# Modulation dots on VectorE, and the operand splits, stores and squares of two stages rearranged, in a two-block fp32 kernel

## The chip, the cores and the metric

The kernel runs on one core of one Trainium2 chip. The time is that of one execution on the device, in microseconds; shorter is better. Beside the runs without a profile there is one profiled execution, from which every instruction's start and duration is known.

## The reference, cut to what matters

Two blocks follow each other on an input of 1024 rows (time) by 1024 channels, all in fp32. In the first block a vector c modulates the normalised input, one projection feeds three branches (pooling, a short convolution, a long convolution), and the branches are gated, summed and projected:

```python
mod = (c_act @ w_ada + b_ada)[:, None, :]
shift, scale, gate = jnp.split(mod, 3, axis=-1)
u = layer_norm(x) * (1 + scale) + shift
proj = u @ w_in + b_in
...
y_a = y_a * pool_scale * jax.nn.silu(a_g)
y_b = b_b * causal_dwconv(b_c * b_h, sc_w, sc_b) * jax.nn.silu(b_g)
h_c = causal_dwconv(c_a * jax.nn.sigmoid(c_b), cf_w, cf_b)
y_c = jax.nn.silu(layer_norm(h_c, cf_ln_g, cf_ln_b)) * jax.nn.silu(c_g)
g_m = jax.nn.sigmoid(merge).reshape(bsz, slen, N_BRANCH, D_MODEL)
m = (g_m[:, :, 0] * (y_a @ w_branch[0])
     + g_m[:, :, 1] * (y_b @ w_branch[1])
     + g_m[:, :, 2] * (y_c @ w_branch[2]))
out = m @ w_out
return layer_norm(ALPHA * x + gate * out, ln_g, ln_b)
```

The second block (attention and a spatial gate) is not touched, except for the last product of its conv-gated MLP, which closes the program:

```python
gate, val = jnp.split(zc, 2, axis=-1)
return (jax.nn.silu(gate) * val) @ w_down
```

Here the gated value is 1024 by 2816, so it is 22 tiles of 128 channels, and `w_down` is 2816 by 1024.

## The kernel before, in words

**Products.** Every fp32 product is made of three TensorE products of split operands. `hilo` casts an operand to a short form on ACT (the hi part, line 165) and subtracts that from the operand on DVE (the lo part, through `tt`, line 159). `mm3` (through `mul`, line 143) then issues hi by hi, hi by lo and lo by hi. One weight tile of 128 channels needs 2 halves of 512 columns by 8 k-tiles by 3 products, 48 matmuls. `act` (line 156) is any ACT function, `stt` (line 162) a fused DVE operation, `flip` (line 146) a transposition on TensorE.

**Order.** The program is a list of slots, written by hand. For each slot the instructions are issued in the order `pre`, `mm`, background tasks (as many from the queue `bgq` as the slot's number `bg` says), `epi`. Each engine and each DMA queue works through its own instructions in this order and waits where a semaphore says so. Weights come through SP's queue into tiles `wr` (two of them, line 247) and are split into `wh` and `wl` some slots ahead (`dma_ahead`, `split_ahead`). A tile name with a ring (`bufs`) is given out again when its last reader is done; the instruction that fills it, a DMA's issue too, waits for that.

**Start** (`start`, from line 552). The input is normalised into eight tiles (`ln_norm`, line 604). Then, for each k-tile of 128 channels, `dot(k)` forms two values per channel, shift and scale, as a row of `w_ada` times the vector, summed: the first with a multiply on POOL (line 644) and a sum and a bias on ACT (`dot_sum`), the second with one DVE instruction (`ada_dot`, line 542, which takes product and sum together, and a second short instruction that reads the accumulator). `prep(k, h)` transposes half h of the k-tile, makes u on ACT and splits it into tiles of U (the names `A` in the profile, line 661 for the cast), and `mac` multiplies three weights by it.

**Long convolution** (`conv_tasks`). A channel tile's 31 taps run on DVE beside the products of later tiles, from p, the gated and padded input, into h. `stats` then stores h, squares it on ACT into an `e` tile (a ring of two, `n_e`; later of one), and two accumulating DMAs on POOL's queue add h and the square into hs and hq. The `e` tiles are used by the epilogues as well (`epi_store`: an activation from PSUM into `e` and a store on SP).

**Passage to the branches.** After the pooling products (`pool_slot(3)` to `pool_slot(0)`, with projection tiles for the merge gates between) the memory of the pool stage is given back (`open_q`) and the branch stage begins. Before its first product it needs y of the second branch: eight tiles from HBM (`yb_sp`), each split (`split_y`) into the big buffers B0 and B1. The first four are fetched to free places when the last paired projection ends (`end`), the last four in `open_q` through tiles `ld` (line 1043). The last two merge tiles leave through `epi_store` (line 836), pool 0's two results through tiles `s`.

**Branches** (`branch(n, d, bg)`). Twenty-four products, n in the order 1, 0, 2, of one weight tile each. The epilogue multiplies PSUM by the gate tile g (a ring of three, loaded from `mg_sp` one branch ahead by `load_g`), adds the sum so far from HBM (`mi<-m_sp`) and stores it on SP (`m_sp<-g`, line 1163), except in the last round. Background tasks make the dots for the gate (first four) and the y tiles of the next n (`prep_y`).

**Second projection** (`down`, from line 1956). The 2816 by 1024 product is done by seven products of half-size blocks in place of eight (Winograd's form of Strassen's scheme). With W1 and W2 the upper and lower 11 tiles of `w_down`, S and T are sums of blocks, of the gated value and of the weights. Seven products p, in the order 1, 5, 2, 6, 7, 3, 4, have 11 units each, one for each k-tile f, and each unit is 12 matmuls (4 banks by 3). For unit u, `step(u)` issues `prep(u + 3)` (sums on DVE, then the split of x and y), `load_sum(u + 9)` (DMAs that fill or accumulate T, the accumulating ones on POOL's queue), `load(u + 7)` (on SP: y into a ring `yr` of four, line 2018, and a tile of the gated value `A<-g_sp`, line 2024), one of the eight loads of the residual x2 in units 13 to 20 (`B<-x_sp`, line 2122), and two background tasks. Four units after a product ended `results(p)` queues its DVE additions into x2 and w, five for each of four banks for p = 6.

Of the kernel before, what the change touches and what calls it, by code (L numbers as in the profile page):

```python
# [22 lines left out]
P = 128  # L23
# [83 lines left out]
class Kernel:  # L107
# [437 lines left out]
    def start(self):  # L545
# [4 lines left out]
        def first():  # L550
# [72 lines left out]
            self.split_ahead(1)  # L623
            dot_sum(0)
            prep(0, 0)
# [7 lines left out]
            dot(1)  # L633
            dot_sum(1)
            prep(1, 0)
# [5 lines left out]
        def dot(k):  # L641
            if k < NK:
                w = st["ada"][2 * k]
                nc.gpsimd.tensor_tensor(w, w, st["cb"], ALU.mult)
                self.ada_dot(8 + k, st["ada"][2 * k + 1], st["cb"])

        def dot_sum(k):
            w, m = st["ada"][2 * k], self.mod[:, k:k + 1]
            self.act(w, w, AF.Identity, accum=m)
            self.act(m, m, AF.Identity, bias=self.par("b_ada", k))  # L650

# [20 lines left out]
        def mm(*ws):  # L672
            steps = [(k, h) for k in range(1, NK) for h in range(2)]
            for i, s in enumerate(steps):
                if i + 2 < len(steps):
                    k, h = steps[i + 2]
                    if h == 0:
                        dot_sum(k)
                    prep(k, h)
                    if h == 0:  # L680
                        dot(k + 1)
                if s[0] < NK - 1:
                    for j in range(3):
                        mac(*s, j)
# [26 lines left out]
    def block1(self):  # L711
# [8 lines left out]
        def conv_tasks(j, p):  # L720
# [10 lines left out]
            def stats():  # L731
                h = T["h"]
                nc.sync.dma_start(h_sp[j], h)
                sq = e_tile()
                self.act(sq, h, AF.Square)
# [96 lines left out]
        def epi_store(ct, func, sp, i):  # L832
            def one(ps, k):
                e = e_tile()
                self.act(e, ps, func, bias=self.bias_in(ct + k))
                nc.sync.dma_start(sp[i + k], e)
            return lambda x, y: [Task(0, lambda: one(x, 0)),
                                 Task(0, lambda: one(y, 1), 4 if self.n_e == 1 else 0)]
# [118 lines left out]
        def pool_slot(g):  # L957
            s = {}

            def pre():  # L960
                while self.bgq:
                    self.bgq.popleft()()
                pairs.flush()
                if g == 0:
                    self.open_right("ws")
                    self.resume()
                    self.dma_ahead()
                    for j in range(4):
                        split_y(1, j)
                    self.split_ahead(1)  # L970
# [13 lines left out]
            def one(c):  # L984
                if g:
                    e = e_tile()
                else:
                    e = self.c1.tile([P, 1040], F, tag="s", name="s", bufs=2)[:, 0:1024]
                self.act(e, s["ps"][c], AF.Identity, scale=self.par("pool_scale", 2 * g + c))
                (nc.sync if g else nc.gpsimd).dma_start(ya_sp[2 * g + c], e)  # L990

            def epi():
                pairs.todo = [Task(0, lambda c=c: one(c), c + 1) for c in range(2)]
                if g == 0:
                    pairs.flush()

# [51 lines left out]
        def open_q():  # L1048
# [8 lines left out]
            T["cb"] = self.c1.tile([P, 1024], F, name="cb2")  # L1057
            for j in range(4, 8):
                load_y(1, j)
            for j in (1, 2):  # L1060
# [50 lines left out]
        def branch(n, d, bg):  # L1111
# [37 lines left out]
            def epi():  # L1149
# [12 lines left out]
                else:  # L1162
                    nc.sync.dma_start(m_sp[d], g)

# [5 lines left out]
        for n in (1, 0, 2):  # L1170
            for d in range(8):
                branch(n, d, 2 if n == 1 else 1)
                if n == 1 and d in (1, 2):
# [790 lines left out]
    def down(self):  # L1964
# [42 lines left out]
        def load(u):  # L2007
# [5 lines left out]
            y = T  # L2013
            if p == 7:
                y = st["T3"][u % 6]
            elif p in (1, 2, 3):
                y = st["ring"].tile([P, H], F, tag="yr", name="yr", bufs=4)
                fetch(y, {1: W1[:, lo], 2: W2[:, lo], 3: W2[:, hi]}[p])
            g = None
# [7 lines left out]
        def load_sum(u):  # L2027
# [6 lines left out]
            if p == 5:  # L2034
                fetch(T, W1[:, lo])
                more(T, W1[:, hi])
# [7 lines left out]
        def prep(u):  # L2044
# [14 lines left out]
            out = []  # L2059
            for x, n in ((src, "x"), (y, "y")):  # L2060
                t = [st["ring"].tile([P, H], R, tag=n + c, name=n + c, bufs=PREP + 1) for c in "hl"]
                self.hilo(*t, x)
                out.append(t)
            st["op", u] = out

# [9 lines left out]
        def results(p):  # L2075
# [6 lines left out]
            for b in range(4):  # L2082
# [7 lines left out]
                elif p == 6:  # L2090
                    add(w, ps, ALU.subtract)
                    add(t21, ps)
                    add(t21, p1)
                    add(t12, w)
                    add(t22, w)
                else:
                    o, op, t, cs = {2: (t11, ALU.add, b, lo), 7: (t22, ALU.subtract, 4 + b, hi),
                                    3: (t12, ALU.add, b, hi), 4: (t21, ALU.add, 4 + b, lo)}[p]
                    add(o, ps, op)
                    tasks.append(lambda t=t, cs=cs: store(t, cs))  # L2100
            if p == 6:
                tasks[:] = tasks[0::5] + tasks[1::5] + tasks[2::5] + tasks[3::5] + tasks[4::5]
            return tasks

        def step(u):
            p, f = units[u]

            def pre():
# [9 lines left out]
                if u == half + 2:  # L2118
                    st["x"] = self.big("B0", F)
                if half + 2 <= u < half + 10:  # L2120
                    t = u - half - 2
                    nc.sync.dma_start(st["x"][:, t], self.x2_sp[t])
# [106 lines left out]
```

## Time and profile before

| | us |
|---|---|
| median of three runs (2690.15 to 2691.99) | 2691.73 |
| the profiled execution's own time | 2690.44 |
| its span, first to last instruction | 2688.6 |
| PE busy | 2618.4 |
| DVE busy | 1861.9 |
| ACT busy | 980.6 |
| POOL busy | 157.4 |

In the profile PE is TensorE, DVE VectorE, ACT ScalarE, POOL GpSimd and SP the engine that issues most DMAs. A row of a timeline has start, duration, engine, line, operation, output<-input, shape and count; a bracket at its end says how long the engine stood idle before it and what released it. A row of windows has the stretch, its length, PE's busy time with the number of matmuls, the granted TensorE clock as a share of full speed, the mean busy share of the DMA engines and the rate in GB/s. A row of waits has who waited, for whom, the total in us, how often, and the longest. The stages by time are: start to 48, projections and the long convolution to about 577, then the pool stage, passage 1023 to 1062, branches from there to about 1310, the second block, and the second projection from 2453 to the end.

### The profile page before, as it was taken

The page shows a single profiled execution, that of the slowest core. Times are in us where ns is not written, and L with a number is a line of the kernel's source. Part 1 is how long each engine was busy: PE and PEld are TensorE (multiplying, and loading weights), DVE is VectorE, ACT ScalarE, POOL GpSimd, SP SyncE. Part 2 cuts the span into 40 slices and gives each one's busy share as a digit, 9 for nine tenths or more (in the row PEclk, how much of TensorE's full clock was granted, in tenths as well). Part 3 has the DMA queues.
Part 4 walks back from the last instruction along what each step waited for, and adds up shares of the span by engine and source line. Part 5 has one row for each costly group of instructions (what it writes and reads, how often), then busy time and mean ns, then how long its engine had stood idle before and what let it go on. Part 6 is the DMA issues. An engine that isn't in the chain of part 4 may idle for free.

```text
span 2688.6 us, 29545 instructions
## 1 busy us (share of the span) xinstructions
PE 2618.4 (97%) x11688; PEld 2142.2 (80%) x11688; DVE 1861.9 (69%) x2141; ACT 980.6 (36%) x1284; POOL 157.4 (6%) x178
## 2 busy tenths in 40 slices
PE   5999999999999998999999999999999999999998
PEld 3888888888888886877787788888788888887786
DVE  7788988989887664666474255536637788885576
ACT  6322233333343343222243255542323334343333
POOL 4000000000000000000042100000000000000220
PEclk9999999999999998999999999999999999999999
DMA  6112232232242225776432122113532222217964
GB/s 236 55 63 79 79 102 86 102 102 102 94 164 98 98 103 206 278 288 234 134 134 87 63 79 79 55 32 119 177 116 79 86 93 72 94 55 239 274 151 147
DMA packets 104396, 331.97 MB, mean 123 GB/s; under 512 B 11713, under 2 KB 12225, under 8 KB 104258
## 3 DMA queue, kind: packets, MB, share of 16 engines
q1 hardware_dynamic: 95474, 309.65, 32.6%
q0 software_dynamic: 8784, 20.45, 4.1%
q8 instruction: 91, 1.49, 0.2%
q14 instruction: 47, 0.39, 0.0%
HBM read 247.21 MB, written 75.50 MB: 120 GB/s over the span
## 4 chain that ended last, share of the span: by engine, by line
PE 63%; issue 15%; DMA 9%; DVE 9%; ACT 3%; SPq 1%; POOL 1%; DVEq 0%; ACTq 0%; POOLq 0%
PE pp L143 61%; DMA ld<-h_sp 1%; DVE h L162 1%; DMA A<-g_sp 1%; DMA B<-x_sp 1%; DMA hs<-h 1%; DVE wl L159 1%; DVE g L159 1%; PE pm L143 1%; DVE A L159 1%; PE pp L146 1%; DVE sums L159 1%; PE pm L146 1%; DVE B L159 1%; DMA adag<-in_ada 1%
## 5 line engine op out<-in xcount | busy, mean ns | idle before, releaser
L143 PE MATMUL pp<-A,wh 128*128 128x512 f32 x2432 | 769.6, 392 | 14.3 <-DVE A L159 9.1
L143 PEld LDWEIGHTS pp<-A,wh 128*128 128x128 f32 x2432 | 454.4, 188 | 116.2 <-DVE A L159 10.9
L143 PE MATMUL pp<-A,wl 128*128 128x512 f32 x1296 | 506.0, 390 | 1.8 <-DVE wl L159 1.8
L143 PE MATMUL pp<-B,A 128*128 128x512 f32 x1676 | 487.7, 390 | 1.2 <-DVE B L159 1.1
L143 PE MATMUL pp<-A,w 128*128 128x512 f32 x1664 | 439.6, 390 | 2.8 <-ACT two L456 1.3
L143 PE MATMUL pp<-B,w 128*128 128x512 f32 x1136 | 374.7, 389 | 0.0
L143 PEld LDWEIGHTS pp<-B,A 128*128 128x128 f32 x1676 | 313.9, 188 | 68.0 <-DVE B L159 2.3
L143 PEld LDWEIGHTS pp<-A,w 128*128 128x128 f32 x1664 | 311.7, 188 | 70.6 <-DVE pp L159 3.8
L162 DVE SCALAR_TENSOR_TENSOR h<-p,par_t,h 128x1024 f32<-128x1024 f32 x240 | 308.6, 1286 | 4.7
L143 PEld LDWEIGHTS pp<-A,wl 128*128 128x128 f32 x1296 | 243.8, 188 | 54.2 <-DVE wl L159 3.5
L143 PE MATMUL pp<-B,wh 128*128 128x512 f32 x800 | 264.7, 395 | 14.3 <-ACT B L165 6.6
L159 DVE TENSOR_TENSOR wl<-wr,wh 128x1024 fp32r<-128x1024 f32 (+1 forms) x120 | 142.5, 1188 | 177.5 <-ACT wh L165 173.8
L143 PEld LDWEIGHTS pp<-B,w 128*128 128x128 f32 x1136 | 213.2, 188 | 44.2
L143 PEld LDWEIGHTS pp<-B,wh 128*128 128x128 f32 x800 | 151.4, 190 | 48.8 <-ACT B L165 7.4
L165 ACT CAST wh<-wr 128x1024 fp32r<-128x1024 f32 (+1 forms) x120 | 118.5, 989 | 187.6 <-PE pp L143 158.1
L162 DVE SCALAR_TENSOR_TENSOR z<-pp,par_t,z 128x1023 f32<-128x1023 f32 x88 | 112.6, 1280 | 48.3 <-ACT z L156 47.3
L143 PE MATMUL pp<-yh,xh 128*128 128x512 f32 x308 | 122.3, 397 | 7.1 <-ACT yh L165 7.1
L143 PE MATMUL pp<-A,A 128*128 128x512 f32 x324 | 126.6, 391 | 0.9 <-DVE A L159 0.6
L143 PE MATMUL pp<-yl,xh 128*128 128x512 f32 x308 | 122.8, 399 | 3.9 <-DVE yl L159 3.8
L143 PE MATMUL pp<-B,wl 128*128 128x512 f32 x320 | 126.0, 394 | 0.0
L373 ACT CAST w<-raw 128x1024 fp32r<-128x1024 f32 x50 | 52.6, 1053 | 200.5 <-PE pp L143 148.5
L143 PE MATMUL pp<-yh,xl 128*128 128x512 f32 x308 | 121.2, 394 | 0.0
(278 smaller groups left out, 3150.8 us busy)
## 6 DMA issues: line engine op xcount, KB each, us to landing
raw<-in_w_in SPq DMA_DIRECT2D x66, 512.0 KB, 4.1
wr<-in_w_in SPq DMA_DIRECT2D x63, 512.0 KB, 3.5
raw<-in_w_up SPq DMA_DIRECT2D x34, 512.0 KB, 5.3
mg_sp<-e SPq DMA_DIRECT2D x24, 512.0 KB, 4.2
wr<-in_w_br SPq DMA_DIRECT2D x24, 512.0 KB, 6.0
g<-mg_sp SPq DMA_DIRECT2D x24, 512.0 KB, 5.6
A<-g_sp SPq DMA_DIRECT2D x44, 256.0 KB, 6.2
g_sp<-z SPq DMA_DIRECT2D x21, 512.0 KB, 3.0
```

Source lines behind the costliest of these rows:

```text
L143: return self.nc.tensor.matmul(*a, **k)
L146: self.nc.tensor.transpose(*a)
L159: return self.nc.vector.tensor_tensor(out, a, b, op)
L162: self.nc.vector.scalar_tensor_tensor(out, a, s, b, op0, op1)
L165: self.nc.scalar.copy(hi, src)
L373: self.nc.scalar.copy(t.__dict__[which][0], src)
```

## The change

It has three parts.

*Start.* `dot(k)` is now two `ada_dot` on DVE; the POOL multiplies, the ACT sums and `dot_sum` go.

*Convolution to branches.* The square of h goes into p, whose taps are done, and no longer into an `e` tile. In `epi_store` the last two merge tiles use an `e` and an `s` tile, and their stores go to POOL's queue. In `pool_slot(0)` the splits of y 0 to 3 are issued ahead of the last pair's epilogues, the four late y tiles are loaded right after the first weights into the big buffer A0, which is free by then, and pool 0's two epilogues write to A0 and become background tasks of the first branch (its `bg` is 4). The stores of m in `branch` go to POOL's queue.

*Second projection.* Product 1 fetches its y straight into T, so that product 5 no longer fetches the same W1 tile again. The x2 loads move from units 13 to 20 to units 20 to 27. `prep` splits y ahead of x. Product 6's results are 12 additions instead of 20: four (adding w to t12) move to product 3's results, and four (adding p1 to t21) to product 2's.

```diff
@@ start @@
         def dot(k):
             if k < NK:
-                w = st["ada"][2 * k]
-                nc.gpsimd.tensor_tensor(w, w, st["cb"], ALU.mult)
-                self.ada_dot(8 + k, st["ada"][2 * k + 1], st["cb"])
+                for n in range(2):
+                    self.ada_dot(8 * n + k, st["ada"][2 * k + n], st["cb"])
-
-        def dot_sum(k):
-            w, m = st["ada"][2 * k], self.mod[:, k:k + 1]
-            self.act(w, w, AF.Identity, accum=m)
-            self.act(m, m, AF.Identity, bias=self.par("b_ada", k))
...
@@ stats @@
-                sq = e_tile()
+                sq = p[:, 0:1024]
@@ epi_store @@
-                e = e_tile()
+                last = sp is mg_sp and i == 22
+                if last and k:
+                    e = self.c1.tile([P, 1040], F, tag="s", name="s", bufs=2)[:, 0:1024]
+                else:
+                    e = e_tile()
                 self.act(e, ps, func, bias=self.bias_in(ct + k))
-                nc.sync.dma_start(sp[i + k], e)
+                (nc.gpsimd if last else nc.sync).dma_start(sp[i + k], e)
@@ pool_slot @@
+                if g == 0:
+                    for j in range(4):
+                        split_y(1, j)
                 pairs.flush()
                 if g == 0:
                     self.open_right("ws")
                     self.resume()
                     self.dma_ahead()
-                    for j in range(4):
-                        split_y(1, j)
+                    t = T["free"] = self.big("A0", F)
+                    for j in range(4, 8):
+                        T["ld"][1, j] = t[:, j]
+                        nc.sync.dma_start(t[:, j], yb_sp[j])
...
-                    e = self.c1.tile([P, 1040], F, tag="s", name="s", bufs=2)[:, 0:1024]
+                    e = T["free"][:, c]
...
                 if g == 0:
-                    pairs.flush()
+                    self.bgq.extend(pairs.todo)
+                    pairs.todo = []
@@ open_q @@
-            for j in range(4, 8):
-                load_y(1, j)
@@ branch @@
-                    nc.sync.dma_start(m_sp[d], g)
+                    nc.gpsimd.dma_start(m_sp[d], g)
...
-                branch(n, d, 2 if n == 1 else 1)
+                branch(n, d, 4 if n == 1 and d == 0 else 2 if n == 1 else 1)
@@ down: load, load_sum @@
-            if p == 7:
+            if p == 1:
+                fetch(T, W1[:, lo])
+            elif p == 7:
                 y = st["T3"][u % 6]
-            elif p in (1, 2, 3):
+            elif p in (2, 3):
...
             if p == 5:
-                fetch(T, W1[:, lo])
                 more(T, W1[:, hi])
@@ down: prep @@
-            for x, n in ((src, "x"), (y, "y")):
+            for x, n in ((y, "y"), (src, "x")):
@@ down: results @@
                     add(t21, ps)
-                    add(t21, p1)
-                    add(t12, w)
                     add(t22, w)
...
+                    if p == 3:
+                        add(o, w)
                     add(o, ps, op)
                     tasks.append(lambda t=t, cs=cs: store(t, cs))
+                    if p == 2:
+                        add(t21, p1)
@@ down: step @@
-                if half + 2 <= u < half + 10:
-                    t = u - half - 2
+                if 2 * half - 2 <= u < 2 * half + 6:
+                    t = u - 2 * half + 2
```

How the instructions move on an engine is shown at three places, as line, operation, output<-input and shape. First DVE in the start, right after the last normalisation, before; `A_201<-u` is the lo part of u, `B_161` a tile of `w_ada`:

```order
L542 ISA B_161,mod<-B_161,cb,bada_76 128x1024
L542 ISA mod 128x1
L159 TENSOR_TENSOR wl<-wr,wh 128x1024
L159 TENSOR_TENSOR A_201<-u,A_202 128x512
L159 TENSOR_TENSOR wl<-wr,wh 128x1024
L159 TENSOR_TENSOR A_201<-u,A_202 128x512
L159 TENSOR_TENSOR w2l<-w_164,w2h 128x1024
L542 ISA B_161,mod<-B_161,cb,bada_76 128x1024
```

and the same place now:

```order
L542 ISA B_161,mod<-B_161,cb,par_t 128x1024
L542 ISA mod 128x1
L542 ISA B_161,mod<-B_161,cb,bada_76 128x1024
L542 ISA mod 128x1
L159 TENSOR_TENSOR wl<-wr,wh 128x1024
L159 TENSOR_TENSOR A_201<-u,A_202 128x512
L159 TENSOR_TENSOR wl<-wr,wh 128x1024
L159 TENSOR_TENSOR A_201<-u,A_202 128x512
L159 TENSOR_TENSOR w2l<-w_164,w2h 128x1024
L542 ISA B_161,mod<-B_161,cb,par_t 128x1024
```

Each k has one more dot on DVE, ahead of the lo parts. Second ACT at the passage, before; `raw` and `sums` hold y 0 to 3, `ld` y 4 to 7, `wh<-wr` are branch weights:

```order
L156 ACTIVATE e<-pp,par_t 128x1024 x2
L165 CAST B_6558<-raw 128x1024 x2
L165 CAST B_6558<-sums 128x1024 x2
L165 CAST wh<-wr 128x1024 x2
L156 ACTIVATE s<-pp,par_t 128x1024 x2
L165 CAST B_6558<-ld 128x1024 x4
```

and now, with y 4 to 7 in `A_6544`:

```order
L165 CAST B_6520<-raw 128x1024 x2
L165 CAST B_6520<-sums 128x1024 x2
L156 ACTIVATE e<-pp,par_t 128x1024
L156 ACTIVATE s<-pp,par_t 128x1024
L165 CAST wh<-wr 128x1024 x2
L165 CAST B_6520<-A_6544 128x1024 x4
L156 ACT_TABLE_LOAD
L156 ACTIVATE cb_6596<-cb_6596 128x1024
L156 ACTIVATE A_6544<-pp,par_t 128x1024 x2
```

The casts of y come ahead of the two merge epilogues, and pool 0's two epilogues behind the casts of the late tiles. Third DVE in the second projection where product 3 is prepared, before; `B_16323` is x2, `A_15809` S and `A_16008` the memory of g, p1 and w:

```order
L159 TENSOR_TENSOR A_15809<-A_15809,A_16008 128x512
L159 TENSOR_TENSOR xl<-A_15809,xh 128x512
L159 TENSOR_TENSOR yl<-yr,yh 128x512
L159 TENSOR_TENSOR B_16323<-B_16323,A_16008 128x512 x2
L159 TENSOR_TENSOR A_15809<-A_15809,A_16008 128x512
```

and now:

```order
L159 TENSOR_TENSOR A_15780<-A_15780,A_15972 128x512
L159 TENSOR_TENSOR yl<-yr,yh 128x512
L159 TENSOR_TENSOR xl<-A_15780,xh 128x512
L159 TENSOR_TENSOR B_16272<-B_16272,A_15972 128x512 x2
L159 TENSOR_TENSOR A_15780<-A_15780,A_15972 128x512
```

The split of y now lies between the sum and the split of x.

More of the change, by code (lines that the diff above doesn't have):

```diff
@@ L623, in first @@
             self.split_ahead(1)
-            dot_sum(0)
             prep(0, 0)
@@ L633, in first @@
             dot(1)
-            dot_sum(1)
             prep(1, 0)
@@ L676, in mm @@
                     k, h = steps[i + 2]
-                    if h == 0:
-                        dot_sum(k)
                     prep(k, h)
@@ L2013, in load @@
             y = T
-            if p == 7:
+            if p == 1:
+                fetch(T, W1[:, lo])
+            elif p == 7:
                 y = st["T3"][u % 6]
-            elif p in (1, 2, 3):
+            elif p in (2, 3):
                 y = st["ring"].tile([P, H], F, tag="yr", name="yr", bufs=4)
-                fetch(y, {1: W1[:, lo], 2: W2[:, lo], 3: W2[:, hi]}[p])
+                fetch(y, W2[:, lo if p == 2 else hi])
             g = None
@@ L2063, in prep @@
                 out.append(t)
-            st["op", u] = out
+            st["op", u] = out[::-1]
         def macs(u, banks):
@@ L2098, in results @@
                                     3: (t12, ALU.add, b, hi), 4: (t21, ALU.add, 4 + b, lo)}[p]
+                    if p == 3:
+                        add(o, w)
                     add(o, ps, op)
                     tasks.append(lambda t=t, cs=cs: store(t, cs))
-            if p == 6:
-                tasks[:] = tasks[0::5] + tasks[1::5] + tasks[2::5] + tasks[3::5] + tasks[4::5]
+                    if p == 2:
+                        add(t21, p1)
+            if p in (2, 6):
+                tasks[:] = tasks[0::3] + tasks[1::3] + tasks[2::3]
             return tasks
```

## The prediction

> **What bounds the kernel now.** The page's first part comes first, because it says which engine could be the bound at all.
>
> ```profile
> span 2688.6 us, 29545 instructions
> PE 2618.4 (97%) x11688; PEld 2142.2 (80%) x11688; DVE 1861.9 (69%) x2141; ACT 980.6 (36%) x1284; POOL 157.4 (6%) x178
> ```
>
> PE (TensorE) is busy for 2618.4 of 2688.6 us, so about 70 us of idle time, and some time at a reduced clock, is all that a change can win which leaves PE's work alone; this one does (11688 matmuls before and after). The second view is PE's busy time by stretches, cut where PE stands still.
>
> ```profile
> core 0: us, PE busy (x), PEclk, DMA share, GB/s
> 0.00:48.00 48.00, 17.60 (x44) 1.00 0.84 329
> 1023.00:1062.00 39.00, 25.63 (x88) 0.82 0.64 230
> 1140.00:1240.00 100.00, 96.93 (x423) 1.00 0.78 284
> 2513.00:2541.00 28.00, 21.49 (x73) 0.88 1.04 305
> 2541.00:2615.00 74.00, 74.00 (x328) 1.00 0.67 151
> 2615.00:2655.00 40.00, 35.93 (x140) 1.00 0.65 181
> ```
>
> In 2541:2615 PE never waits: 74.00/328 = 0.2256 us is the floor of a 512-column matmul. What a stretch loses is its length less its matmuls by that: 1023:1062 loses 39 − 88 × 0.2256 = 19.1, 1140:1240 4.6, 2513:2541 11.5, 2615:2655 8.4 us. The first 48 us hold little PE work. The change touches each of these five places, so the rest of the trace was read there, in the timeline and in the waits.
>
> **Start (dots on DVE).** The rows are from the timelines of POOL, DVE, ACT and PE; the column after the start is the duration.
>
> ```profile
> 20.71 11.68 POOL L644 TENSOR_TENSOR B<-B,cb 128x1024 f32<-128x1024 f32 x4
> 19.22 0.80 DVE L604 TENSOR_SCALAR B<-B,sm 128x1024 f32<-128x1024 f32 x1
> 20.78 2.82 DVE L604 TENSOR_SCALAR B<-B,sm 128x1024 f32<-128x1024 f32 x1 [0.77 <-POOL sm L601]
> 42.21 3.37 DVE L542 CUSTOM_DVE_ANT_0 B<-B,cb,bada 128x1024 f32<-128x1024 f32 x1
> 47.17 0.69 DVE L159 TENSOR_TENSOR A<-u,A 128x512 fp32r<-128x512 f32 x1 [1.58 <-ACT A L661]
> 47.78 1.28 DVE L542 CUSTOM_DVE_ANT_0 B<-B,cb,bada 128x1024 f32<-128x1024 f32 x1
> 45.71 0.78 ACT L156 ACTIVATE u<-pm,mod 128x512 f32<-128x512 f32 x1 [12.67 <-DVE mod L542]
> 39.04 0.79 PE L143 MATMUL pp<-A,wh 128*128 128x512 f32 x1 [4.39 <-DVE A L159]
> 47.91 0.50 PE L143 MATMUL pp<-A,wh 128*128 128x512 f32 x1 [0.23 <-DVE A L159]
> ```
>
> While POOL multiplies (from 20.71, without a gap for eight tiles), the same DVE dot takes 3.37 us that takes 1.28 once POOL is done, and the last normalisation takes 2.82 against 0.80. With the multiplies gone POOL runs nothing there, so I take the short durations for every DVE instruction of the start.
>
> Now the chain with short durations. The last normalisation ends at 20.78 + 0.80 = 21.6; two dots of k = 0 at 1.28 end by 24.2. ACT then makes u (0.78), its cast (about 0.62), two weight casts (about 1.04 each) and the second half: 28.8. DVE has wl, ul, wl, ul and w2l between, each as soon as its cast is there, and ends w2l at 30.0; the two dots of k = 1 end at 32.6, u and cast at 34.0, ul at 34.7. PE has 18 matmuls and 8 transposes of k = 0 from 26.3 on; at a pitch of 0.43 us (the rows from 39 to 43 us are twice as slow as the floor) it is done at about 36.5. So the first matmul of k = 1 moves from 47.9 to about 37: a gain of **10.5** (8 to 12, as PE's clock is slow for more or less of it). Beyond it PE has 18 matmuls and 8 transposes per k, about 5 us, and DVE 2 × 1.28 + 2 × 0.69 = 3.9: two dots instead of one still hide under PE. What they cost if not is 0.2 us a k.
>
> **Squares into p.** After the last merge tiles of the convolution part an epilogue waits for a tile that the accumulating DMA of the squares still reads.
>
> ```profile
> 575.08 1.11 ACT L156 ACTIVATE e<-pp,par_t 128x1024 f32<-128x1024 f32 x1 [4.56 <-DMA hq<-e]
> 576.72 3.02 PE L143 MATMUL pp<-A,w 128*128 128x512 f32 x12 [1.33 <-ACT two L456]
> ```
>
> Squares no longer take an e tile, so the 4.56 us on ACT go, and with them PE's 1.33. The tile p they now hold is not written again until the next channel's gating, some 60 us later, which covers the accumulating DMA (the waiter above found it late by 4.56 us only). Gain **1.3** (0 to 1.5).
>
> **Passage to the branches.** SP, ACT, DVE and PE in the order of their start:
>
> ```profile
> 1028.93 4.18 SPq L836 DMA_DIRECT2D mg_sp<-e  x2
> 1033.21 8.45 SPq L247 DMA_DIRECT2D wr<-in_w_br  x4
> 1042.23 10.28 SPq L1043 DMA_DIRECT2D ld<-yb_sp  x4
> 1032.67 1.98 ACT L165 CAST B<-raw 128x1024 fp32r<-128x1024 f32 x2
> 1037.73 1.05 ACT L165 CAST wh<-wr 128x1024 fp32r<-128x1024 f32 x1 [1.19 <-DMA wr<-in_w_br]
> 1051.86 1.04 ACT L165 CAST B<-ld 128x1024 fp32r<-128x1024 f32 x1 [9.79 <-DMA ld<-yb_sp]
> 1052.93 1.23 DVE L159 TENSOR_TENSOR B<-ld,B 128x1024 fp32r<-128x1024 f32 x1 [11.62 <-ACT B L165]
> 1038.83 1.22 PE L143 MATMUL pp<-B,wh 128*128 128x512 f32 x2 [6.33 <-ACT wh L165]
> 1052.95 0.79 PE L143 MATMUL pp<-B,wh 128*128 128x512 f32 x1 [5.66 <-ACT B L165]
> 1061.59 0.62 PE L143 MATMUL pp<-B,wh 128*128 128x512 f32 x2
> ```
>
> PE ends pool 0 at 1038.83 − 6.33 = 1032.5 and waits for the first branch weight, whose DMA stood on SP behind the two merge stores. It waits again, 5.66 us, for y tile 4 of 8, because the four late y loads can be issued only after pool 0 has been stored out of the memory they land in. Between them it runs at half clock (0.82 in the row of the stretch). With the stores on the GpSimd queue SP is free from about 1018: weights land near 1022, the y loads go into A0, free when the last merge product has read it (about 1027), and land from 1030 to 1036 at the pace of the y loads above.
>
> On ACT the four casts of y 0 to 3 come first (B free at 1023.3, so 4 × 1.0 to 1027.5), then two epilogues (1.1 each) to 1030, two weight casts to 1032, four casts of the late tiles to 1036. DVE follows with 1.23 a tile: y lo 1032.5, weights lo 1033.7 and 1034.9, late tiles 1039.7. PE ends pool 0 at 1032.5, waits 0.9 for the first wl, then runs 48 matmuls of branch 1.0 in 10.8: 1044.2, where before branch 1.1 began at 1061.59, the last row. That is 17.4; I take **17** (13 to 18.5: 13 if the y loads land at the 10.28 us pace above from a start 4 us later, 18.5 if no weight wait is left).
>
> **Stores of m on the GpSimd queue.** The landing times of the stores and loads of tile ya_sp (min/median/max; its longest, 8.7, is of the two stores that POOL issues), and a DMA row of the page, whose last number is the median to landing:
>
> ```profile
> DMA to landing us min/median/max: 2.6/4.6/8.7
> g<-mg_sp SPq DMA_DIRECT2D x24, 512.0 KB, 5.6
> ```
>
> The sixteen stores wait on SP for each branch's sum, and loads queue behind them; in 1140:1240 PE loses 4.6 us, mostly for y products whose loads came late. Without the stores SP reaches its loads up to a branch earlier. I take **2.5** (4.5 if all of it goes, −2 if landings like the 8.7 hold g tiles now and then). The Trainium skill, page "DMA: Bandwidth & Descriptors", section "Issuing engines are not separate DMA queues", speaks against this: all issuers share the same 16 DMA engines, and only issue time is saved; by it, if the late loads of this stretch are late by bandwidth, the term is 0 and the time 2642.5. The DMA share of 0.78 there, below the 1.04 of 2513:2541, is why I don't take it so.
>
> **Second projection.** Seven products of 11 units each, 12 matmuls a unit, 2.71 us at the floor. The first two rows are the x2 loads (tile x_sp from 2480 to 2550) and their landing; then ACT's waits from 2510 to 2540, one wait of PE, and the DVE timeline of product 3.
>
> ```profile
> L2122 SPq DMA_DIRECT2D B<-x_sp x8: 319/320/320, 2491.3 to 2525.9; - x8
> DMA to landing us min/median/max: 12.0/15.0/15.7
> ACT xh L165 <- DMA A<-g_sp: 19.0, 6, 4.9
> 2517.79 0.50 PE L143 MATMUL pp<-yh,xh 128*128 128x512 f32 x1 [1.04 <-ACT yh L165]
> 2630.08 0.69 DVE L159 TENSOR_TENSOR xl<-A,xh 128x512 fp32r<-128x512 f32 x1 [0.76 <-ACT xh L165]
> 2630.69 0.68 DVE L159 TENSOR_TENSOR yl<-yr,yh 128x512 fp32r<-128x512 f32 x1
> 2631.29 1.29 DVE L159 TENSOR_TENSOR B<-B,A 128x512 f32<-128x512 f32 x2
> 2632.50 0.69 DVE L159 TENSOR_TENSOR A<-A,A 128x512 f32<-128x512 f32 x1
> ```
>
> *Product 2* (2513:2541) is DMA-bound: a DMA share of 1.04 at 305 GB/s, and loads wait in a full queue (x2 tiles land after 15 us, ACT waits 19.0 us for g). Ahead of that point the change takes away 11 × 256 KB (W1 read once) and moves eight x2 loads of 512 KB behind it by seven units: 7 MB, at 305 GB/s 23 us of transfer, against 11.5 lost. The loads for products 6 and 7 behind it have slack in 2541:2615 (0.67). I take **11.3** (6 if half the stall stays behind the accumulating DMAs, 11.9).
>
> *Product 3* loses 8.4 to 8.7. Here DVE is in a cycle: 0.76 idle until x is cast, then from start to start xl 0.61, yl 0.60, two adds 1.21 and the sum for the next unit 0.69, together 3.87 a unit. With y split first, yl fills the idle time: 3.26 with two adds, 2.05 with none, and 8 of the 20 adds leave product 6's results, so only some six units carry two. 6 × (3.26 − 2.71) = 3.3 us of lag stays within the three units (8 us) prepared ahead. Gain **8.5** (6 to 8.7). Product 1's y straight into T saves its two short stalls: **0.9** (0 to 1).
>
> **Sum.** 10.5 + 1.3 + 17 + 2.5 + 11.3 + 8.5 + 0.9 = 52.0. The profiled execution took 2690.44 (span 2688.6 and 1.84 around it): 2690.4 − 52.0 = 2638.4. The median of the runs is 2691.73, 1.3 above it: 2639.7, predicted **2640.0**. A difference of 0.2%, 5.4 us, is what a measurement tells from no change.
>
> **Rivals.** (a) The passage is partly given back: with branch 1.0 done at 1044, branch 1.2 needs gate tiles and the sums of h, loaded on SP behind everything else; if they come at the old distance, PE stalls about 8 us there: 2648. For it: cb and ada loads stood after 1055 before; against it: by my chain they land near 1046, 4 us ahead of need. Chance 0.12. (b) In product 2 the accumulating DMAs, not the bytes, set the pace, and half the stall stays: 2646. The share above 1 in 2513:2541 speaks for bytes. Chance 0.12. (c) POOL's multiplies do not slow DVE; then DVE gains nothing at the start and the two dots in a row replace one: term 0 to 2, 2649. Against it stand 3.37 and 1.28. Chance 0.06. (d) The slower side: m's stores on POOL's queue land late. The g ring has three tiles, so a load of g waits on SP for the store three branches back, with branch weights behind it. Three branches are 3 × 48 × 0.2256 = 32.5 us; less a load of 5.6 and two DVE steps of 1.23, a store may take 24 us. At 40 us each third branch is 16 us late: 16 × 16/3 = 85 lost, 2725. At about 34 the loss is 52 and the time unchanged. The slowest known landing, 8.7, is far from that. The Trainium skill, page "SBUF — State Buffer", section "Who interferes with whom", names a way to it: a DMA issued by GpSimd can be starved by VectorE of the port time in which its descriptors are made; no row here but the 8.7 bears on it. Slower 0.03, same 0.02. The forecast itself has 0.65.
>
> All the upper ends of the terms give 12 + 1.5 + 18.5 + 4.5 + 11.9 + 8.7 + 1 = 58.1, so 2633.6; (a) and (b) together 2654. Range **2633.0 to 2656.0**. All cases but (d) are faster: 0.95 faster, 0.02 same, 0.03 slower.
>
> **What would show it.** Right: DVE dots of 1.3 us from 21.6 on and the first k = 1 matmul near 37; one PE wait of about 1 us after pool 0 and branch 1.1 near 1044 less the 12 us won before; no PE wait in product 2, and a DVE cycle under 3.3 us in product 3. Wrong: long dots without POOL, PE waits for gate tiles in branch 1.2, ACT still waiting for g in product 2, m_sp landings above 20 us.

## The result, and the profile after

The changed kernel takes 2631.66 us (median of four runs, 2631.33 to 2632.98) against 2690.94 us for the kernel before beside it. The ratio is 0.9783, 95% interval 0.9768 to 0.9799: 59.3 us less. Forecast were 2640.0 us and a range from 2633.0, so the direction and the order of size were right, and the time lies 1.3 us below the range. The page after begins so:

```profile
span 2629.8 us, 29512 instructions
## 1 busy us (share of the span) xinstructions
PE 2599.1 (99%) x11688; PEld 2139.3 (81%) x11688; DVE 1855.9 (71%) x2157; ACT 972.5 (37%) x1260; POOL 144.0 (5%) x188
```

PE has the same 11688 matmuls. Its busy time is 19 us less all the same: a matmul that runs slowly counts with its longer duration, and the stretches with a granted clock of 0.82 and 0.88 are gone. The stretches that lost time before, now (the bounds have moved with the time won):

```profile
core 0: us, PE busy (x), PEclk, DMA share, GB/s
0.00:38.00 38.00, 18.57 (x51) 1.00 0.95 372
1005.00:1030.00 25.00, 23.75 (x104) 1.00 0.70 261
1030.00:1106.00 76.00, 76.00 (x338) 1.00 0.90 331
1106.00:1206.00 100.00, 100.00 (x443) 1.00 0.78 283
2470.00:2490.00 20.00, 20.00 (x90) 1.00 1.01 324
...
2564.00:2596.00 32.00, 32.00 (x143) 1.00 0.83 260
```

From 1030 on PE is busy without a gap in each of them, and the clock is 1.00 in all rows. The DMA share beside product 2 (2470:2490) is still 1.01: the engines are as full as before, but nothing waits for them.

As both kernels issue the same PE instructions in the same order, the start of the n-th matmul can be subtracted between the two traces. The difference is what has been won up to that place, and its steps are the stages' gains:

| stage | forecast, us | the two traces, us |
|---|---|---|
| start, to k = 1 | 10.5 | 11.3 |
| squares into p | 1.3 | 1.7 near 577, and 0.7 near 624 |
| passage, to the end of branch 1.0 | 17 | 17.5 |
| branches after it | 2.5 | 5.6 |
| not touched: near 933, and the second block | 0 | 0.8 |
| product 1 | 0.9 | 1.0 |
| product 2 | 11.3 | 11.9 |
| product 3 | 8.5 | 8.7 |
| sum | 52.0 | 59.2 |

How far one pair of traces can be trusted is shown by the six experiments below that leave the passage and the branches as before. Against the trace of before they lose 0.3 to 2.7 us over the passage, and over the branches they come out between 2.1 us worse and 2.3 better. So the split into 17.5 and 5.6 is uncertain by some 2 us. The sum of the two, 23.1, is firmer: against each of those six it is 23.0 to 26.5, where the forecast had 19.5.

The places one by one. DVE in the start, from the last normalisation on:

```profile
21.53 0.81 DVE L604 TENSOR_SCALAR B<-B,sm 128x1024 f32<-128x1024 f32 x1 [0.77 <-POOL sm L601]
22.25 1.28 DVE L542 CUSTOM_DVE_ANT_0 B<-B,cb,par_t 128x1024 f32<-128x1024 f32 x1
...
23.46 1.28 DVE L542 CUSTOM_DVE_ANT_0 B<-B,cb,bada 128x1024 f32<-128x1024 f32 x1
```

The dots take 1.28 us and the normalisation 0.81, where they took 3.37 and 2.82. Two dots now end sooner than one did.

The passage, on SP, ACT and PE:

```profile
1013.39 1.82 SPq L968 DMA_DIRECT2D A<-yb_sp  x4
1019.59 1.47 SPq L247 DMA_DIRECT2D wr<-in_w_br  x2
...
1024.25 1.05 ACT L165 CAST B<-A 128x1024 fp32r<-128x1024 f32 x1 [1.44 <-DMA A<-yb_sp]
...
1019.62 0.50 PE L143 MATMUL pp<-B,wl 128*128 128x512 f32 x1 [0.51 <-DVE wl L159]
```

The four late loads are issued within 1.82 us instead of 10.28, and in place of the two waits of 6.33 and 5.66 us there is one of 0.51 (PE starts with the hi parts and waits only for the first lo part of the weights). After the start of branch 1.0 PE does not wait again in the stage.

DVE while product 3 is prepared, after the last addition for product 6:

```profile
2565.55 0.69 DVE L159 TENSOR_TENSOR A<-A,A 128x512 f32<-128x512 f32 x1
2566.15 0.69 DVE L159 TENSOR_TENSOR yl<-yr,yh 128x512 fp32r<-128x512 f32 x1
2566.98 0.69 DVE L159 TENSOR_TENSOR xl<-A,xh 128x512 fp32r<-128x512 f32 x1
2567.59 0.68 DVE L159 TENSOR_TENSOR A<-A,A 128x512 f32<-128x512 f32 x1
```

The sum, yl and xl follow each other with almost no idle time; without additions a unit takes 2567.59 − 2565.55 = 2.04 us, as the forecast's 2.05 has it.

### The profile page after: what moved, and what is told of

It is laid out like the page before. It is cut to its first block, busy times and chain, and to the rows that moved or that the text cites. A ratio compares the mean times of both kernels' runs of the same rounds, so it can differ in the third digit from the quotient of the medians.

```text
span 2629.8 us, 29512 instructions
## 1 busy us (share of the span) xinstructions
PE 2599.1 (99%) x11688; PEld 2139.3 (81%) x11688; DVE 1855.9 (71%) x2157; ACT 972.5 (37%) x1260; POOL 144.0 (5%) x188
## 4 chain that ended last, share of the span: by engine, by line
PE 91%; DVE 4%; ACT 2%; issue 1%; DMA 1%; POOL 1%; SPq 0%; DVEq 0%; ACTq 0%; POOLq 0%
PE pp L143 89%; PE pm L143 1%; PE pm L146 1%; PE pp L146 1%; DVE wl L159 1%; ACT oj L156 0%; DVE z L162 0%; DVE sums L159 0%; DVE A L159 0%; DVE B L159 0%; DVE h L162 0%; POOL ox L1293 0%; ACT wh L165 0%; DVE ox L159 0%; DMA B<-in_xt 0%
```

## The experiments

Each kernel was timed beside the kernel before on the same chip; the medians of before were 2689.43, 2691.42 and 2692.11 in the three groups of four. Differences are against that median, if nothing else is said. A difference to the changed kernel compares two groups; there the difference of the two ratios to before and the one between the traces are given too.

### Each part alone

The first takes from the change the start and the squares:

```diff
-                nc.gpsimd.tensor_tensor(w, w, st["cb"], ALU.mult)
-                self.ada_dot(8 + k, st["ada"][2 * k + 1], st["cb"])
+                for n in range(2):
+                    self.ada_dot(8 * n + k, st["ada"][2 * k + n], st["cb"])
...
-                sq = e_tile()
+                sq = p[:, 0:1024]
```

> The kernel before with two parts of the change: both dots on VectorE in the start, and the square of h in p. Theory (the multiplies on POOL slowed every VectorE instruction with two operands): start 11.4 us earlier as in the two traces, squares 1.3, in all 12.7 less than before, ratio about 0.9953; the POOL-free dots take 1.28 us. Rival (VectorE is slow there for another reason, and a second dot lengthens its chain): dots near 3.3 us and 0 to 3 us gained. The 0.9 us that the trace after also gains near 612 us is put on neither part; if it shows here it belongs to the squares.

Measured: 2677.19 us, 12.2 less, ratio 0.9950 (0.9936 to 0.9964). In its trace the start wins 12.0, the place near 577 another 1.7 and the place near 624 another 0.5. So the last belongs to these two parts, most likely the squares, whose `e` tiles the forecast had followed only as far as the first epilogue that waits.

The second is the passage alone (the diff's hunks in `epi_store`, `pool_slot`, `open_q` and the number of background tasks), the third one word:

```diff
-                    nc.sync.dma_start(m_sp[d], g)
+                    nc.gpsimd.dma_start(m_sp[d], g)
```

> The kernel before with only the passage changed (y splits first, late y tiles into A0, last two merge stores on POOL's queue, pool 0's epilogues later); the stores of m stay on SP. Theory A (the 5.5 us won in the branch stage come from m's stores): 17.6 us less than before, all by branch 1.1, ratio 0.9935. Theory B (they come from the passage, whose late y tiles no longer take the ring that later loads use): 21 to 23 us less, ratio 0.992. If branch 1.2 waits for gate tiles, 10 to 13 less.

> The kernel before with one word changed: the sixteen stores of m on POOL's queue. Theory A (SP waits 125.7 us in all for the sums of the branches before it may store, and loads stand behind): 5 to 5.5 us less than before, ratio 0.998. Theory B (the passage brought it): 0 to 1.5 less. By the skill's rule that issuers share the same engines: 0. If POOL's stores land late: slower.

Measured: the passage alone 2678.39 us, 11.0 less, ratio 0.9959 (0.9946 to 0.9971); the stores alone 2686.86 us, 2.6 less, ratio 0.9992 (0.9983 to 1.0, so this alone is not clear of no change). The stores alone lie between theory A (5 to 5.5) and theory B (0 to 1.5). For the passage alone neither holds; it falls into the third case of its expectation, 10 to 13 less. Together the two parts win 23.1 in the trace after; alone they add up to 13.6.

The trace of the stores alone has this row for the stretch in which PE lost 4.6 us before:

```profile
1140.00:1240.00 100.00, 100.00 (x443) 1.00 0.77 278
```

So all of that loss goes, at the same places as in the trace after (near 1149, 1168 and 1239; 4.8 us in both). Against it stands a new PE wait of 1.41 us near 1103, and the passage came 2.4 us later in this execution, as in others that leave it as it was.

The trace of the passage alone shows where the rest is. Branch 1.1 does come some 17 us sooner (16.6 at the end of branch 1.0, in a profile that was 0.9 behind until then), and then this happens, on SP, DVE and PE:

```profile
1041.90 0.93 SPq L1105 DMA_DIRECT2D adag<-in_ada  x2
1057.25 0.33 SPq L1171 DMA_DIRECT2D m_sp<-g  x1
1057.63 1.92 SPq L1105 DMA_DIRECT2D adag<-in_ada  x2
...
1063.87 1.28 DVE L542 CUSTOM_DVE_ANT_0 adag<-adag,cb,par_t 128x1024 f32<-128x1024 f32 x1 [5.51 <-DMA adag<-in_ada]
...
1074.40 0.69 DVE L198 COPY wide<-inv 128x1024 f32<-128x1024 f32 x1 [1.79 <-POOL inv L174]
...
1075.24 3.76 PE L143 MATMUL pp<-cst,wide 128*128 128x128 f32 x16 [4.92 <-DVE wide L198]
```

SP comes to the first store of m at about 1043 and stands there until branch 1.0's sum is made, 1057.25. The next two `adag` tiles, which the dots for the gate read, are queued behind it and issued at 1057.63. DVE waits 5.51 us for them with its dots, and in its queue behind the dots lies the chain of the long convolution's norm, which ends in the tile `wide`. PE waits 4.92 us for that, and then runs its next matmuls at about twice their time. In the kernel before the same store, tile and product stood so:

```profile
1070.43 0.33 SPq L1163 DMA_DIRECT2D m_sp<-g  x1
1086.46 0.69 DVE L198 COPY wide<-inv 128x1024 f32<-128x1024 f32 x1 [1.79 <-POOL inv L174]
1087.31 2.02 PE L143 MATMUL pp<-cst,wide 128*128 128x128 f32 x16 [0.32 <-DVE wide L198]
```

There PE waited only 0.32 us for `wide`. With the passage alone PE is ready for it some 16.7 us sooner, but the tile is made only 12.1 us sooner (1074.40 against 1086.46). The lead over the kernel before falls from 16.7 to 9.9 us at this place. It is the forecast's rival (a) in kind: PE stalls because loads come late on SP, near the size that it gave (8 us). The loads are those of the gate's dots, and the experiments further below show that moving the stores prevents it.

The fourth is the second projection alone (all hunks in `down`):

> The kernel before with only the second projection changed. Theory (the terms of the two traces add up): product 1 about 1, product 2 12.0, product 3 8.7, in all 21.8 us less than before, ratio 0.9919. Rival (accumulating DMAs set product 2's pace and the rest of the change only moved them): 12 to 16 less, with ACT still waiting for g in product 2.

Measured: 2668.61 us, 20.8 less, ratio 0.9922 (0.9910 to 0.9935). No unit of the projection takes more than 2.72 us. This part stands by itself. The four runs add up to 46.6 us, against 59.3 for the whole change; most of the missing 12.7 is won only by the passage and the stores together, as the next two runs show.

### The stores of m, given the passage

Two kernels start from the changed one. In the first all sixteen stores are back on SP, in the second only the first is left on POOL's queue:

```diff
-                    nc.gpsimd.dma_start(m_sp[d], g)
+                    (nc.gpsimd if n == 1 and d == 0 else nc.sync).dma_start(m_sp[d], g)
```

> The changed kernel with the stores of m back on SP. Theory (from the run with the passage alone: SP's wait for the first branch's sum, ahead of the store, holds the loads of the next two gate tiles; VectorE waits for them with the spread of the norm behind, and PE waits 4.9 us and then runs slow): about 2643, 11 to 12 us above the changed kernel, with a PE wait for tile wide of about 5 us. Theory of the prediction (the stores are worth their 2.5 us alone, whatever the passage does): 2634. By the skill's rule that only issue time is saved: 2632.

> The changed kernel with only the first of the sixteen stores of m on POOL's queue, fifteen on SP. Theory (that first store blocks the gate loads): the PE wait for wide is gone, and only the 2 to 5 us of the late y loads are lost: 2634 to 2637. If the whole series of stores matters for it: 2640 or more.

Measured: 2644.29 us with all on SP, ratio to before 0.9824 (0.9811 to 0.9838), and 2637.87 us with only the first on POOL's queue, 0.9799 (0.9785 to 0.9812). Against the changed kernel that is 12.6 and 6.2 slower by the medians, 11.0 and 4.3 by the ratios, and 13.1 and 7.6 in the traces, all of it between 1045 and 1270 (the second run's trace is of its slowest execution; its median lies 0.9 above the expected range). So about half hangs on the very first store and half on the fifteen others. The longest waits of PE between 1030 and 1270 with all on SP (total, times, longest):

```profile
PE pp L143 <- DVE wide L198: 4.8, 1, 4.8
PE pp L143 <- ACT B L165: 0.9, 1, 0.9
PE pp L143 <- DVE A L159: 0.8, 1, 0.8
```

and with only the first on POOL's queue:

```profile
PE pp L143 <- DVE wl L159: 1.4, 1, 1.4
PE pp L143 <- ACT B L165: 0.9, 1, 0.9
PE pp L143 <- DVE B L159: 0.8, 1, 0.8
```

The wait for `wide` is gone with the first store; the short waits for split y tiles (`A`, `B`) stay until the others go too. The changed kernel has no PE wait in that window. So the stores are worth 2.6 us in the old surroundings (0 to 4.6 by the interval) and 11 to 13 in the new.

### POOL beside DVE

Here the changed kernel keeps both dots on DVE, and POOL multiplies a tile that is not used, eight times; nothing waits for it:

```diff
+            junk = c.tile([P, 1024], F, tag="junk", name="junk", bufs=1)
+            for _ in range(8):
+                nc.gpsimd.tensor_tensor(junk, st["cb"], st["cb"], ALU.mult)
             dot(0)
```

> The changed kernel with eight multiplies on POOL into an unused tile as the start's dots begin; both dots stay on VectorE and nothing waits for POOL. Theory (POOL's two-operand reads slow VectorE's): VectorE's dots take 3.3 us again for as long as POOL runs (24 us), and the start is 9 to 13 us longer: 2641 to 2645. Rival (the chain through POOL and ACT was the loss, not the rate of VectorE): 2632 with dots of 1.28.

Measured: 2644.09 us, 12.4 above the changed kernel by the medians and 11.3 by the ratios; ratio to before 0.9825 (0.9812 to 0.9838). In the traces the start loses 11.6. POOL and DVE:

```profile
20.88 20.12 POOL L624 TENSOR_TENSOR junk<-cb 128x1024 f32<-128x1024 f32 x8
...
20.95 2.37 DVE L604 TENSOR_SCALAR B<-B,sm 128x1024 f32<-128x1024 f32 x1 [0.77 <-POOL sm L601]
23.24 2.91 DVE L542 CUSTOM_DVE_ANT_0 B<-B,cb,par_t 128x1024 f32<-128x1024 f32 x1
...
42.00 1.27 DVE L542 CUSTOM_DVE_ANT_0 B<-B,cb,par_t 128x1024 f32<-128x1024 f32 x1
```

As long as POOL runs (to 41.0) a dot takes 2.91 us, afterwards 1.27. All that the start won is lost again although no instruction waits for POOL's result: it was the rate of DVE, and not the chain through POOL and ACT. The Trainium skill, page "SBUF — State Buffer", section "Who interferes with whom", has the rule that a VectorE instruction with two operands in SBUF contends with a GpSimd instruction that reads SBUF; the run agrees, with 2.91 us against 1.27.

### The second projection taken apart

Four of its edits by ones and twos, on the kernel before: the x2 loads later; the split of y first; both; W1's left half fetched once. The time that PE loses in each product is what its units take above 2.72 us:

| kernel | time, us | less by | product 1 | 2 | 6, 7 | 3 |
|---|---|---|---|---|---|---|
| before (profile) | | | 1.0 | 11.9 | 0 | 8.7 |
| x2 loads later | 2686.30 | 5.1 | 1.7 | 1.0 | 4.9 | 9.1 |
| W1 once | 2678.80 | 13.3 | 0 | 0 | 0 | 8.4 |
| y first | 2679.52 | 12.6 | 0.4 | 8.1 | 0 | 0 |
| y first, x2 later | 2671.08 | 21.0 | 1.6 | 0 | 0 | 0 |
| all of the stage | 2668.61 | 20.8 | 0 | 0 | 0 | 0 |

The ratios to before are 0.9982 (0.9974 to 0.9991), 0.9949 (0.9937 to 0.9962), 0.9954 (0.9941 to 0.9966) and 0.9923 (0.9909 to 0.9936), in the order of the rows.

```diff
-                if half + 2 <= u < half + 10:
-                    t = u - half - 2
+                if 2 * half - 2 <= u < 2 * half + 6:
+                    t = u - 2 * half + 2
```

> The kernel before with only the eight x2 loads moved seven units later. Theory (bytes ahead of product 2 in a full DMA): 4.2 MB less there, 13.8 us of transfer at 305 GB/s against a stall of 11.9, so product 2 loses at most 2: 10 to 12 less than before. Rival (accumulating DMAs of W1 and W2 set the pace): 0 to 5 less. As the x2 loads now share the time of product 2's own loads, a stall of a few us may come after it.

The whole gain, 5.1 us, misses the 10 to 12 of the theory and is close to the rival's 0 to 5, but not by the rival's way: product 2's stall goes, all but 1.0 us, and 6 us are lost again behind it. The stretches of this run, from product 2 on:

```profile
2515.00:2541.00 26.00, 25.61 (x112) 1.00 1.06 319
2541.00:2570.00 29.00, 29.00 (x130) 1.00 0.42 117
2570.00:2600.00 30.00, 29.47 (x128) 1.00 0.88 202
2600.00:2651.00 51.00, 45.11 (x171) 1.00 0.73 187
```

Two units at the end of product 2 wait for loads, which uses up the lead that the three prepared units give. In the old order a unit costs DVE 2.66 us without additions, so it wins back 0.06 a unit at most, and each addition from there on falls on PE: first in products 6 and 7, then in product 3.

```diff
-            for x, n in ((src, "x"), (y, "y")):
+            for x, n in ((y, "y"), (src, "x")):
```

> The kernel before with only the split of y ahead of x in the second projection. Theory (VectorE's cycle of 3.87 us a unit is set by its wait for the cast of x; with y in it 3.26 with two additions and 2.05 without, so the lead of three units absorbs all 20 additions): product 3's 8.7 us are gone, product 2's 11.9 stay: 8 to 9 less than before. Rival (the eight additions taken out of product 6's results are what counts): 2 to 4 less.

12.6 us less, more than expected. The two stretches of products 2 and 3:

```profile
2515.00:2541.00 26.00, 21.72 (x81) 0.93 1.07 325
...
2612.00:2655.00 43.00, 43.00 (x192) 1.00 0.68 201
```

Product 3's loss is gone, with all 20 additions still in place: fewer additions are not needed for it. That product 2 loses 8.1 instead of 11.9, with the same bytes ahead of it, was not foreseen, and no run separates why.

> The kernel before with the split of y ahead of x and the eight x2 loads seven units later, W1 still fetched twice and the additions as before. Theory (the late loads removed product 2's stall and lost it again because VectorE could not regain its lead; with the new order it can): 20 to 21 us less than before, nearly all of what the whole change of this stage gives (20.8). Rival (fetching W1 once and the fewer additions are needed too): 12 to 15 less, with stalls of PE left in products 2, 7 or 3.

21.0 us less, as the theory says and as the whole stage gives: with the new order DVE regains its lead, and what the late loads cost in the run before is gone. The two stalls of product 1 (1.6 us here) are left.

> The kernel before with W1's left half fetched once, straight into T, and nothing else. Theory (bytes ahead of product 2: 2.9 MB less, 9.4 us at 305 GB/s): product 2's stall falls from 11.9 to about 2.5, the two stalls of product 1 (1.0) go; as in the run with late x2 loads VectorE's debt then takes about 6 back in products 7 and 3: in all 3 to 5 less. If the order of loads in SP's queue sets it and not their bytes: product 2's stall stays, 1 less.

Here the expectation was wrong, 13.3 us less instead of 3 to 5. Its stretches of products 2 and 3:

```profile
2504.00:2530.00 26.00, 26.00 (x116) 1.00 1.07 314
...
2603.00:2643.00 40.00, 35.96 (x140) 1.00 0.67 180
```

Product 2 loses nothing, product 3 what it lost before, and no debt appears in between, because no load is late and the lead is kept. The 2.9 MB saved are 9.4 us at 305 GB/s and remove 11.9, so bytes alone do not account for it; the loads of product 1, no longer held by the ring of four, also start sooner, and the two were not separated.

### A version that starts sooner

PE's largest idle time left lies in the start, and the dots of k = 0 do not need the normalised input:

```diff
                 if t:
                     ln_norm(t - 1)
+                if t in (5, 7):
+                    self.ada_dot(8 * (t // 7), st["ada"][t // 7], cb)
...
-            dot(0)
             self.split_ahead(1)
```

> The changed kernel with the two dots of k = 0 put into the two gaps of 0.77 us in which VectorE waits for POOL between the last normalisations. Theory: the last normalisation ends about 1 us later, the two dots behind it (2.4 us) are gone, and the first products start 1.5 us earlier: 2630, ratio to the changed kernel 0.9994. Rival (the first tile of w_ada lands too late for the first gap, or PE's slow pitch takes it back): 2631 to 2632.

Measured: 2630.15 us (2629.97 to 2630.40), ratio to before 0.9769 (0.9756 to 0.9783); the changed kernel's runs, in another group, were 2631.33 to 2632.98, ratio 0.9783 (0.9768 to 0.9799). The medians differ by 1.5 us, as expected, but the intervals overlap, so the times alone don't show a gain. The traces do for the start: the first product starts at 24.5 instead of 26.3, and this kernel is 2.5 us ahead after it. Of these 1.2 are lost near 1905, in a part that both kernels share, and 1.3 are left at the end.

## Why the prediction was right or wrong

*What bounds the kernel* held: PE's idle time at five places. Of it only some in the start and 0.51 us in the passage are left.

*Start* held: 11.3 (12.0 alone) against 10.5, within 8 to 12. Its premise, POOL's work slowing DVE, is shown by the run that puts POOL's work back. The slow pitch of PE in this stage, 0.43 us a matmul, is read from durations; the clock column has 1.00 for 0:48, so why the matmuls are slow there stays open.

*Squares* was 1.3 and came to 2.4 in the trace, above its upper bound of 1.5: the second place, near 624, was not priced. One reading was too simple: POOL clears 30 columns of p ahead of the next gating, and now does so only when the accumulating DMA has landed (564.3 in the trace after). No wait of PE shows for it.

*Passage*: 17.5 against 17, on the chain that the forecast gave. But its gain is kept only because another part of the change protects it; alone the edit gives 11.0.

*The stores of m* is the step that failed: "I take **2.5** (4.5 if all of it goes, −2 if landings like the 8.7 hold g tiles now and then)". The mechanism was the right one, SP's loads standing behind a store that waits for a branch's sum; the term was too small in two ways. First, it took about half of what the stretch 1140:1240 lost, and all of it goes: PE is busy for 100.00 of 100 us there with the stores alone, and for 100.00 of 100 in 1106:1206 of the trace after. The branches won 5.6 against 2.5, the largest part of what the sum lacks; the upper bound of 4.5 had been read in that one stretch only. Second, it was priced in the trace of before. With the passage changed the same stores cost 11 to 13 us when they are put back on SP, some 7 of them at the product with `wide`, where the forecast had credited the passage with its full 17 as though nothing followed. That the stores alone measured 2.6, next to the 2.5 taken, is luck: it is 4.8 won in the stretch less what that run lost elsewhere, with an interval that reaches 0.

The Trainium skill, page "DMA: Bandwidth & Descriptors", section "Issuing engines are not separate DMA queues", says that all issuers share the same DMA engines and that several of them save only issue time. By that rule the term was 0. The DMA share, 0.78 in 1140:1240 before and in 1106:1206 after, fits the first half of it. What moving the stores saved was no time of issuing but SP's waits ahead of later loads, and that was not small.

*Second projection*: 21.6 against 20.7. Each of the three stalls is gone. For product 3 the forecast's explanation is shown, and the order alone does it; the fewer additions are not needed. For product 2 the bytes are not the whole account: fetching W1 once takes away 9.4 us of transfer and removes 11.9, and y first removes 3.8 with the same bytes. The runs add that the change fixes product 2 twice over (either W1 once, or the late x2 loads with y first).

*The rivals*: (a) is real, and it is the stores' move that prevents it, which the forecast did not connect. (b) fell: no wait is left in product 2. (c) fell. (d) fell: m's stores land after 5.3 us at the median and 8.0 at most, far from 24:

```profile
L1161 POOL DMA_DIRECT2D m_sp<-g x16: 533/533/599, 1043.0 to 1201.7; - x16
...
DMA to landing us min/median/max: 3.2/5.3/8.0
```

*The range* missed by 1.3 us. All terms came out above the value taken, two above their upper bound (squares by 0.9, branches by 1.1), and 0.8 us came from places that the change doesn't touch. The upper ends had been added up to 58.1, and this sum was taken as the far end of the range though those of the squares and the branches were each read at one place only.

## What to carry to other kernels

Price an edit that frees a queue in the surroundings that the other edits make, not in those of the old trace: when compute moves up by 17 us, a load that had slack and does not move up with it has up to 17 us less of it. Where a store that waits for a result stands in the queue that also issues loads, look at which loads are behind it and who reads them, two engines on. A pipeline with a fixed lead pays for each late load for as long as its slowest engine has no spare time per unit, so first give that engine slack (here by an order that fills its own wait), then move loads.

## What the runs showed of the hardware that was not expected

Work on POOL slowed DVE instructions with a single tensor operand as well, as the forecast had read from one row: the normalisation took 2.37 us beside the experiment's multiplies, which nothing waits for, and 0.81 without them. What was new is that DVE's time seems to go with POOL's own pace: beside the multiplies before, 11.68/4 = 2.9 us a tile, a dot took 3.4, beside those of the experiment, 20.12/8 = 2.5 us a tile, it took 2.91. Two points do not make it a rule.

A wait of PE cost more than its length. With all stores of m on SP PE waited 4.8 us for `wide` and lost 7.3 against the changed kernel at this place. With the passage alone the 16 short matmuls behind the same wait took 3.76 us, where 16 took 2.02 before, and the granted clock was 0.50 from 1075.2 to 1079.
